# The output projection of a hybrid decoder layer in 512-column products by channel group, with the second half's residual rows placed behind the first half's norm

## The chip, the cores and the metric

The kernel runs on one core of a Trainium2 chip. The metric is the device time of one execution in microseconds (us). The core has a matrix engine (PE, whose weight loads are listed as PEld), a vector engine (DVE), an activation engine (ACT), a general engine (POOL) and a queue engine that issues DMAs (SP). Each engine works through its own list of instructions in order; an instruction waits there until the ones it depends on, on other engines, are done.

## The reference

One layer of a decoder with 1024 tokens and 1024 channels, all in float32. Cut to what matters here:

```python
proj = x @ w_in + b_in
q, k, v, a, gate = split(proj)                       # 512, 128, 128, 512, 512 columns
y_attn = sliding_window_gqa(q, k, v, sinks, table)   # 8 heads of 64, window 128, (1024, 512)
y_conv = conformer_conv_group(a, gate, ...)          # GLU, causal conv of 31, LayerNorm, silu, (1024, 512)
y   = concat([rms_norm(y_attn, attn_out_gain), rms_norm(y_conv, conv_out_gain)])
mix = y @ w_out + b_out                              # (1024, 1024) @ (1024, 1024)
x1  = layer_norm(alpha * x + mix, ln1_g, ln1_b)      # alpha = 2 ** 0.25
h   = causal_depthwise_conv(x1 @ w_up, ...)          # 5632 columns, conv of 3
g, u = split(h)
x   = layer_norm(alpha * x1 + (silu(g) * u) @ w_down, ln2_g, ln2_b)
```

The RMS norm of each group is one factor per token and one gain per channel. The gains are multiplied into the operands, and the factor per token can be applied after the product, separately for the 512 attention channels and the 512 conv channels.

## The kernel before

The 1024 tokens are worked on in two halves (H = 0 and 1) of 512 tokens, each in four blocks of 128 (t = 0 to 3). Every float32 matrix is split into a high and a low part of a shorter type: for weights, ACT casts the high part (line 236) and POOL subtracts it from the original (line 238). A product is then three matmuls: high by high, high by low, low by high.

A half goes through the input projection, the conv group (`conv`, `conv_norm`), the attention (`attn`), the output projection (`out_proj`), the first norm (`ln1`) and the feed-forward part. The conv group's end, `conv_norm`, subtracts the mean over channels (POOL's sums, line 466), multiplies by the deviation's inverse (DVE, line 489), applies silu (ACT, line 490, which needs its function table loaded), and makes the high part (ACT, line 491), the low part (DVE, line 492) and squares (ACT, line 495) for the RMS factor. The attention's units reduce the scores on DVE (line 533), take exponentials on ACT (line 540, another function table, with line 544 for the sinks), split the probabilities (ACT line 562, DVE line 563) and scale and split the result (ACT line 588, DVE line 590).

`out_proj(H)` first loads `b_out` to all partitions and the four rows blocks of x; DVE makes alpha * x + b_out of each (line 646, 128 x 1024), and this is the row block `acc` to which the products are added. Then it goes over four blocks of 256 output columns. For each it loads and splits the attention rows of `w_out` (`wa`, eight DMAs of 64 x 256, because the heads are paired) and the conv rows (`wc`, one DMA). For each t twelve matmuls of 256 columns (lines 661 to 663) make the attention group's product in one half of a PSUM bank, and twelve more (lines 665 to 667) the conv group's in the other half; DVE adds each to `acc` with its factor per token (`sA`, line 671; `sC`, line 673). The banks come from a pair with the tag A. In the first half, `chain` keeps the long products in the order in which they are written.

`ln1(0)` normalises a row block (`layer_norm_rows`: lines 321 and 323 statistics, 315 and 316 inverse root, 334 to 336 the row itself) and `transpose_split` turns it: PE transposes four 128 x 128 pieces into a bank (line 283), ACT casts them to the high part (line 286), DVE subtracts for the low part (line 287). This is done twice for each row block. The up products of the feed-forward part (lines 270, 271 and 273, in `mm3`; convolution and silu in lines 706 to 722) need all four row blocks. `ln1(1)` does the same for the second half in another form (transposes in line 297).

What sets the order: the parts are generators that yield after each piece of work, and a string names which one goes on next:

```python
SCRIPT = ('0hx00j0hxixxiiiggacaaaaaaaaaaaaannnCCaaagagCkCqqaaaqqoAAAoA'
          'AAAAoAAoNAlAlNAlAlNAAAAfAfAAOOOfsOsssffLLLLffff')
```

o is the first half's `out_proj`, l its `ln1`, A and N the second half's attention and conv norm, O and L its `out_proj` and `ln1`, f feed-forward work of the first half, s sums for the later joint stage. From about 498.5 us on both halves go through the feed-forward part together. A scheduler takes the instructions in this order as priorities, works out a schedule with its own cost model, and from it the list of each engine; a dependence added by hand (`add_manual_dep` with the class NoSync) binds only the order.

Of the kernel before, what the change touches and what calls it, by code (L numbers as in the profile page):

```python
# [15 lines left out]
P = 128  # L16
# [53 lines left out]
def hybrid_layer_kernel(  # L70
# [52 lines left out]
    last_tap = [None]  # L123

# [151 lines left out]
    def transpose_split(src, xh, xl, t, key):  # L276
        banks = []
        for q in range(2):
            b = psk(key)
            banks.append(b)  # L280
            for k in range(4):
                kt = q * 4 + k
                nc.tensor.transpose(out=b[:, k * P:(k + 1) * P], in_=src[:, kt * P:(kt + 1) * P], identity=ident)
            bv_ = b.rearrange("p (k t) -> p k t", t=P)
            hd = xh[q][:, :, t * P:(t + 1) * P]
            nc.scalar.copy(out=hd, in_=bv_)
            nc.vector.tensor_tensor(out=xl[q][:, :, t * P:(t + 1) * P], in0=bv_, in1=f(hd), op=ALU.subtract)  # L287
        return banks
# [328 lines left out]
    def wout_rows(c0, q0):  # L617
        def g(raw):
            r = []
            for j in range(4):  # L620
                c = c0 + j
                if c < 4:
                    for k in range(2):
                        rows = slice(k * 256 + c * HD, k * 256 + (c + 1) * HD)
                        r.append((raw[k * HD:(k + 1) * HD, j, :], w_out[rows, q0:q0 + 256]))
            if c0 >= 4:
                r = [(raw, w_out[c0 * P:(c0 + 4) * P, q0:q0 + 256].rearrange("(c p) n -> p c n", p=P))]
            return r
        return g

    def split_wout(c0, q0):
        return split_weights(wout_rows(c0, q0), (P, 4, 256), ("oh", "ol", "or"))
# [4 lines left out]
    def out_proj(H):  # L637
        ych, ycl = yC[H]
        bo = bcast_row(b_out, "bo")
        for t in range(TB):  # L640
# [4 lines left out]
            if XM[H]:  # L645
                nc.vector.scalar_tensor_tensor(out=a, in0=a, scalar=ALPHA, in1=bo, op0=ALU.mult, op1=ALU.add)
# [3 lines left out]
        for q in range(4):  # L650
            wa = split_wout(0, q * 256)
            wc = split_wout(4, q * 256)
            for t in range(TB):
                b = H * TB + t
                cs = slice(q * 256, (q + 1) * 256)
                yah, yal = yA[b]
                ts_ = slice(t * P, (t + 1) * P)
                pa = psk("out%d" % H, (P, 2, 256))
                m = []
                for c in range(4):  # L660
                    m.append(nc.tensor.matmul(out=pa[:, 0, :], lhsT=yah[:, c, :], rhs=wa[0][c], start=c == 0, stop=False))  # L661
                    m.append(nc.tensor.matmul(out=pa[:, 0, :], lhsT=yah[:, c, :], rhs=wa[1][c], start=False, stop=False))
                    m.append(nc.tensor.matmul(out=pa[:, 0, :], lhsT=yal[:, c, :], rhs=wa[0][c], start=False, stop=c == 3))
                for c in range(4):
                    m.append(nc.tensor.matmul(out=pa[:, 1, :], lhsT=ych[c][:, ts_], rhs=wc[0][c], start=c == 0, stop=False))
                    m.append(nc.tensor.matmul(out=pa[:, 1, :], lhsT=ych[c][:, ts_], rhs=wc[1][c], start=False, stop=False))
                    m.append(nc.tensor.matmul(out=pa[:, 1, :], lhsT=ycl[c][:, ts_], rhs=wc[0][c], start=False, stop=c == 3))
                if H == 0:
                    chain(m[0], m[-1])
                a = acc[b][:, cs]  # L670
                nc.vector.scalar_tensor_tensor(out=a, in0=pa[:, 0, :], scalar=sA[H][:, t:t + 1], in1=a,
                                               op0=ALU.mult, op1=ALU.add)
                nc.vector.scalar_tensor_tensor(out=a, in0=pa[:, 1, :], scalar=sC[H][:, t:t + 1], in1=a,
                                               op0=ALU.mult, op1=ALU.add)
            yield

    def ln1(H, g, b):
# [3 lines left out]
        for t in range(TB):  # L681
            a = acc[H * TB + t]
            if H == 0:
                layer_norm_rows(a, g, b, H)
                transpose_split(a, xh, xl, t, "ln0")
# [423 lines left out]
```

## Time and profile before

| | us |
|---|---|
| three runs | 1107.92, 1106.47, 1104.14 |
| median | 1106.47 |
| the profiled execution, its own time | 1105.66 |
| its span | 1103.9 |

Busy time in the span: PE 1047.1 us (95%), DVE 780.9, POOL 660.6, ACT 496.3. A share of 95% is a mean over stages: in some PE is full, in others DVE or a chain through several engines sets the pace. The views used below are the chain of waits (which work was last to end, followed backward), windows (busy time of each engine in a stretch), and timelines (single instructions with start, duration, and in brackets the idle time before them and what ended it). Where the profile groups neighbours, a row has a count (x4) and their busy time together. The second half's held rows of the change are the four of line 646 at 295.66 to 304.87 us.

### The profile page before, as it was taken

To read this page: it belongs to the slowest core of one execution; us is meant where nothing else is said; L and a number is where in the kernel's file an instruction comes from. 1 tells how busy PE (TensorE), PEld (TensorE's weight loads), DVE (VectorE), ACT (ScalarE), POOL (GpSimd) and SP (SyncE) were. 2 spreads that over 40 slices of the span, in tenths; PEclk is the share of its full clock that TensorE was granted. 3 is DMA by queue.
4 is the path that set the end of the run, shared out by engine and by line. 5 is a ranking of instruction groups with operands and counts; after the bars stand their busy time and mean duration, and the time that the engine had idled before them with its cause. 6 is when DMAs were issued, how large, how long until landed. Compare 5 with 4: busy or idle time off the path is not lost.

```text
span 1103.9 us, 14411 instructions
## 1 busy us (share of the span) xinstructions
PE 1047.1 (95%) x5113; PEld 872.3 (79%) x5113; DVE 780.9 (71%) x1426; ACT 496.3 (45%) x949; POOL 660.6 (60%) x564
## 2 busy tenths in 40 slices
PE   7999999988968999989999999999999999999996
PEld 5887778778957999767788787878787887888875
DVE  2999789999997447984747566565747466569666
ACT  4545677653458325662525242423425152442530
POOL 4759687874686555776646363737456463637551
PEclk9999999999968999999999999999999999999999
DMA  6535221423500242231212020211212110233321
GB/s 185 173 79 132 83 57 33 143 69 102 165 20 1 72 139 72 58 101 39 77 39 76 21 77 20 77 38 47 68 39 77 39 58 20 77 115 121 109 96 76
DMA packets 115673, 85.20 MB, mean 77 GB/s; under 512 B 20370, under 2 KB 108049, under 8 KB 115601
## 3 DMA queue, kind: packets, MB, share of 16 engines
q1 hardware_dynamic: 112368, 78.92, 24.2%
q10 hardware_dynamic: 3233, 5.36, 1.4%
q8 instruction: 40, 0.66, 0.3%
q14 instruction: 32, 0.26, 0.1%
HBM read 80.06 MB, written 4.21 MB: 76 GB/s over the span
## 4 chain that ended last, share of the span: by engine, by line
PE 77%; DVE 11%; POOL 4%; DMA 3%; ACT 3%; issue 1%; SPq 0%; POOLq 0%; ACTq 0%; DVEq 0%
PE psA L270 6%; PE psA L271 6%; PE psA L273 6%; PE psS L746 2%; PE psS L748 2%; PE psS L747 2%; PE psS L829 2%; PE psA L829 2%; PE psA L827 2%; PE psS L827 2%; PE psA L826 2%; PE psS L826 2%; PE psS L528 2%; DVE psC L444 1%; PE psA L661 1%
## 5 line engine op out<-in xcount | busy, mean ns | idle before, releaser
L238 POOL TENSOR_TENSOR wl<-raw,wh 128x512 fp32r<-128x512 f32 x196 | 260.1, 1339 | 139.0 <-ACT wh L236 67.4
L236 ACT CAST wh<-raw 128x512 fp32r<-128x512 f32 x196 | 119.2, 619 | 168.3 <-PE psA L271 19.9
L238 POOL TENSOR_TENSOR wl<-ts,wh 128x512 fp32r<-128x512 f32 x64 | 82.5, 1296 | 155.1 <-ACT wh L236 135.3
L444 DVE SCALAR_TENSOR_TENSOR psC<-hconv,const,psC 128x512 f32<-128x512 f32 x196 | 147.3, 752 | 3.5
L270 PE MATMUL psA<-x,wh 128*128 128x512 f32 x336 | 132.7, 395 | 4.4 <-ACT wh L236 3.5
L271 PE MATMUL psA<-x,wh 128*128 128x512 f32 x336 | 132.0, 393 | 1.4 <-DVE x L287 1.4
L236 ACT CAST wh<-ts 128x512 fp32r<-128x512 f32 x64 | 39.4, 622 | 177.4 <-PE psS L748 39.2
L273 PE MATMUL psA<-x,wl 128*128 128x512 f32 x336 | 87.2, 395 | 0.8 <-POOL wl L238 0.8
L270 PEld LDWEIGHTS psA<-x,wh 128*128 128x128 f32 x336 | 63.1, 188 | 19.1 <-ACT wh L236 4.1
L271 PEld LDWEIGHTS psA<-x,wh 128*128 128x128 f32 x336 | 63.1, 188 | 14.6 <-DVE x L287 1.7
L273 PEld LDWEIGHTS psA<-x,wl 128*128 128x128 f32 x336 | 62.4, 188 | 15.3 <-POOL wl L238 1.2
L316 POOL TENSOR_TENSOR tiny<-tiny,const 128x1 f32<-128x1 f32 (+1 forms) x28 | 26.0, 933 | 58.9 <-DVE tiny L315 55.9
L753 DVE TENSOR_TENSOR acc<-psS,acc 128x512 f32<-128x512 f32 x52 | 35.7, 688 | 31.6 <-PE psS L748 31.6
L238 POOL TENSOR_TENSOR ol<-or,oh 128x512 fp32r<-128x512 f32 x32 | 40.7, 1292 | 17.3 <-ACT oh L236 17.3
L826 PE MATMUL psA<-x,wh 128*128 128x512 f32 x112 | 43.6, 389 | 0.0
L827 PE MATMUL psA<-x,wh 128*128 128x512 f32 x112 | 43.6, 389 | 0.0
L826 PE MATMUL psS<-x,wh 128*128 128x512 f32 x112 | 43.6, 389 | 0.0
L827 PE MATMUL psS<-x,wh 128*128 128x512 f32 x112 | 43.6, 389 | 0.0
L865 POOL TENSOR_TENSOR ts<-raw,ts 128x512 f32<-128x512 f32 x32 | 41.9, 1310 | 1.3
L436 POOL TENSOR_TENSOR cp<-cp,cp 128x512 f32<-128x512 f32 x28 | 36.2, 1292 | 8.3 <-ACT cp L432 8.3
L746 PE MATMUL psS<-wh,gh 128*128 128x512 f32 x88 | 34.9, 397 | 6.3 <-ACT gh L726 3.9
L661 PE MATMUL psA<-oh,x 128*128 128x256 f32 x128 | 38.1, 297 | 1.8 <-ACT z L422 1.5
(394 smaller groups left out, 3081.1 us busy)
## 6 DMA issues: line engine op xcount, KB each, us to landing
raw<-in_w_up SPq DMA_DIRECT2D x56, 512.0 KB
raw<-in_w_down SPq DMA_DIRECT2D x28, 512.0 KB
raw<-in_w_in SPq DMA_DIRECT2D x20, 512.0 KB
raw<-in_x SPq DMA_DIRECT2D x8, 512.0 KB
raw<-in_w_in SPq DMA_DIRECT2D x16, 256.0 KB
acc<-in_x SPq DMA_DIRECT2D x8, 512.0 KB
or<-in_w_out SPq DMA_DIRECT2D x64, 64.0 KB
or<-in_w_out SPq DMA_DIRECT2D x8, 512.0 KB
```

What stands on the lines that cost most here:

```text
L236: nc.scalar.copy(out=h, in_=part)
L238: nc.gpsimd.tensor_tensor(out=l, in0=part, in1=f(h), op=ALU.subtract)
L270: m.append(nc.tensor.matmul(out=o, lhsT=wh[kt], rhs=xh[kt], start=kt == 0, stop=False))
L271: m.append(nc.tensor.matmul(out=o, lhsT=wh[kt], rhs=xl[kt], start=False, stop=False))
L273: m.append(nc.tensor.matmul(out=o, lhsT=wl[kt], rhs=xh[kt], start=False, stop=kt == KT - 1))
L444: tap(nc.vector.scalar_tensor_tensor(out=dst if k == KO else total, in0=src, scalar=cdw(k, c), in1=total, op0=ALU.mult, op1=ALU.add))
L661: m.append(nc.tensor.matmul(out=pa[:, 0, :], lhsT=yah[:, c, :], rhs=wa[0][c], start=c == 0, stop=False))
L746: m.append(nc.tensor.matmul(out=o, lhsT=gh[:, tsl], rhs=wh, start=j == 0, stop=False))
L826: m.append(nc.tensor.matmul(out=o, lhsT=wh[k], rhs=xh[k], start=k == 0, stop=False))
L827: m.append(nc.tensor.matmul(out=o, lhsT=wh[k], rhs=xl[k], start=False, stop=False))
L829: m.append(nc.tensor.matmul(out=o, lhsT=wl[k], rhs=xh[k], start=False, stop=k == 3))
L865: nc.gpsimd.tensor_tensor(out=t, in0=x0, in1=x1, op=ALU.subtract)
```

## The change

In `out_proj` the loop over four blocks of 256 columns becomes a loop over the channel group and two blocks of 512 columns: first the conv group's two blocks, then the attention group's two. Each t then has twelve matmuls of 512 columns into one full bank and one DVE eviction of 128 x 512 with that group's factor. The weights come in tiles of 128 x 2 x 512: one DMA for a conv tile, four of 64 x 512 for an attention tile. Per half that makes 192 matmuls instead of 384, 16 evictions instead of 32, and 20 DMAs of `w_out` instead of 36. `transpose_split` also returns its last subtract, and in `out_proj(1)` the four instructions that make alpha * x + b_out must stand behind the last such subtract of `ln1(0)` in DVE's list.

```diff
             bv_ = b.rearrange("p (k t) -> p k t", t=P)
             hd = xh[q][:, :, t * P:(t + 1) * P]
             nc.scalar.copy(out=hd, in_=bv_)
-            nc.vector.tensor_tensor(out=xl[q][:, :, t * P:(t + 1) * P], in0=bv_, in1=f(hd), op=ALU.subtract)
-        return banks
+            i = nc.vector.tensor_tensor(out=xl[q][:, :, t * P:(t + 1) * P], in0=bv_, in1=f(hd), op=ALU.subtract)
+        return banks + [i]
...
     def wout_rows(c0, q0):
         def g(raw):
+            if c0 >= 4:
+                return [(raw, w_out[c0 * P:(c0 + 2) * P, q0:q0 + 512].rearrange("(c p) n -> p c n", p=P))]
             r = []
-            for j in range(4):
-                c = c0 + j
-                if c < 4:
-                    for k in range(2):
-                        rows = slice(k * 256 + c * HD, k * 256 + (c + 1) * HD)
-                        r.append((raw[k * HD:(k + 1) * HD, j, :], w_out[rows, q0:q0 + 256]))
-            if c0 >= 4:
-                r = [(raw, w_out[c0 * P:(c0 + 4) * P, q0:q0 + 256].rearrange("(c p) n -> p c n", p=P))]
+            for j in range(2):
+                for k in range(2):
+                    r0 = k * 256 + (c0 + j) * HD
+                    r.append((raw[k * HD:(k + 1) * HD, j, :], w_out[r0:r0 + HD, q0:q0 + 512]))
             return r
         return g
 
     def split_wout(c0, q0):
-        return split_weights(wout_rows(c0, q0), (P, 4, 256), ("oh", "ol", "or"))
+        hs, ls = [], []
+        for c in (c0, c0 + 2):
+            h, l = split_weights(wout_rows(c, q0), (P, 2, 512), ("oh", "ol", "or"))
+            hs += h
+            ls += l
+        return hs, ls
...
             if XM[H]:
-                nc.vector.scalar_tensor_tensor(out=a, in0=a, scalar=ALPHA, in1=bo, op0=ALU.mult, op1=ALU.add)
+                i = nc.vector.scalar_tensor_tensor(out=a, in0=a, scalar=ALPHA, in1=bo, op0=ALU.mult, op1=ALU.add)
+                if H == 1:
+                    tc.add_manual_dep(i.ins, last_row[0].ins.name, order, reason="rows of one half at a time")
...
-        for q in range(4):
-            wa = split_wout(0, q * 256)
-            wc = split_wout(4, q * 256)
+        for part_, q in ((1, 0), (1, 1), (0, 0), (0, 1)):
+            wh, wl = split_wout(4 * part_, q * 512)
             for t in range(TB):
...
-                pa = psk("out%d" % H, (P, 2, 256))
+                if part_:
+                    yh, yl = [[y[c][:, ts_] for c in range(4)] for y in (ych, ycl)]
+                else:
+                    yh, yl = [[y[:, c, :] for c in range(4)] for y in yA[b]]
+                pa = psk("out%d" % H)
                 m = []
                 for c in range(4):
...
+                    m.append(nc.tensor.matmul(out=pa, lhsT=yh[c], rhs=wh[c], start=c == 0, stop=False))
+                    m.append(nc.tensor.matmul(out=pa, lhsT=yh[c], rhs=wl[c], start=False, stop=False))
+                    m.append(nc.tensor.matmul(out=pa, lhsT=yl[c], rhs=wh[c], start=False, stop=c == 3))
                 if H == 0:
                     chain(m[0], m[-1])
...
-                nc.vector.scalar_tensor_tensor(out=a, in0=pa[:, 1, :], scalar=sC[H][:, t:t + 1], in1=a,
-                                               op0=ALU.mult, op1=ALU.add)
+                a = acc[b][:, q * 512:(q + 1) * 512]
+                s = (sC if part_ else sA)[H]
+                nc.vector.scalar_tensor_tensor(out=a, in0=pa, scalar=s[:, t:t + 1], in1=a, op0=ALU.mult, op1=ALU.add)
             yield
...
-                transpose_split(a, xh, xl, t, "ln0")
+                last_row[0] = transpose_split(a, xh, xl, t, "ln0")[2]
```

In the changed kernel most lines have a number higher by one (287 is 288, 490 is 491, 540 is 541, 722 is 723); the residual rows are line 650 instead of 646, and the evictions line 675 instead of 671 and 673.

The first place where the order of instructions moves is DVE at the end of the first half's output projection, where its evictions (lines 671 and 673) and the first norm's statistics (lines 315, 321, 323) meet. Before (`acc_2114` and the next three are the first half's row blocks, `acc_3463` and the next the second half's):

```order
L671 SCALAR_TENSOR_TENSOR acc_2117<-psA,tiny_60,acc_2117 128x256
L323 BN_AGGR tiny_60<-tiny_60 128x2
L646 SCALAR_TENSOR_TENSOR acc_3463<-acc_3463,bo_3461 128x1024
L673 SCALAR_TENSOR_TENSOR acc_2117<-psA,tiny_60,acc_2117 128x256
L315 TENSOR_SCALAR tiny_60<-tiny_60 128x1
L321 BN_STATS tiny_60<-acc_2120 128x6
L646 SCALAR_TENSOR_TENSOR acc_3466<-acc_3466,bo_3461 128x1024
L671 SCALAR_TENSOR_TENSOR acc_2120<-psA,tiny_60,acc_2120 128x256
L321 BN_STATS tiny_60<-acc_2117 128x6
```

In the changed kernel these four rows stand on DVE at the end of the first norm, behind its last two subtracts (line 288; lines 493 are the conv norm's low parts, 538 and 546 attention):

```order
L288 TENSOR_TENSOR x_97<-psA,x_96 128x4x128
L538 TENSOR_TENSOR tiny_60<-const_61,tiny_60 128x4
L493 SCALAR_TENSOR_TENSOR x_95<-cy_1510,const_61,x_94 128x512
L316 TENSOR_SCALAR tiny_60<-psT 128x1
L493 SCALAR_TENSOR_TENSOR x_95<-cy_1511,const_61,x_94 128x512
L493 SCALAR_TENSOR_TENSOR x_95<-cy_1512,const_61,x_94 128x512
L288 TENSOR_TENSOR x_265<-psA,x_264 128x4x128
L650 SCALAR_TENSOR_TENSOR acc_3239<-acc_3239,bo_3237 128x1024
L650 SCALAR_TENSOR_TENSOR acc_3242<-acc_3242,bo_3237 128x1024
L650 SCALAR_TENSOR_TENSOR acc_3245<-acc_3245,bo_3237 128x1024
L650 SCALAR_TENSOR_TENSOR acc_3248<-acc_3248,bo_3237 128x1024
L546 TENSOR_TENSOR tiny_60<-tiny_60 128x4
```

The four rows moved as one group from among the evictions to behind the last subtract, and three of the conv norm's subtractions now stand ahead of that subtract.

The second place is ACT at the fourth row block's two casts (line 286, now 287, to `x_96` and `x_264`), where the conv norm's silus of the second half begin. Before:

```order
L286 CAST x_96<-psA 128x4x128
L490 ACT_TABLE_LOAD
L490 ACTIVATE cy_1510<-cy_1510,const_61 128x512
L286 CAST x_264<-psA 128x4x128
L686 ACTIVATE acc_2123<-acc_2123 128x1024
L490 ACTIVATE cy_1511<-cy_1511,const_61 128x512
L491 ACTIVATE x_94<-cy_1510,const_61 128x512
L495 ACTIVATE nsq_2938<-cy_1510 128x512
```

In the changed kernel, where the table for silu and two of the silus stand ahead of the first of these casts:

```order
L287 CAST x_96<-psA 128x4x128
L491 ACTIVATE cy_1512<-cy_1512,const_61 128x512
L492 ACTIVATE x_94<-cy_1510,const_61 128x512
L496 ACTIVATE nsq_2714<-cy_1510 128x512
L491 ACTIVATE cy_1513<-cy_1513,const_61 128x512
L492 ACTIVATE x_94<-cy_1511,const_61 128x512
L496 ACTIVATE nsq_2717<-cy_1511 128x512
L541 ACT_TABLE_LOAD
L541 ACTIVATE hank_262,tiny_60<-hank_262,tiny_60 128x256 x2
L492 ACTIVATE x_94<-cy_1512,const_61 128x512
L496 ACTIVATE nsq_2720<-cy_1512 128x512
L287 CAST x_264<-psA 128x4x128
```

Between the two casts one silu with its table load has become two silus, three pairs of lines 492 and 496, and a table load with two exponentials.

More of the change, by code (lines that the diff above doesn't have):

```diff
@@ L123, in hybrid_layer_kernel @@
     last_tap = [None]
+    last_row = [None]
     def tap(i):
@@ L649, in out_proj @@
                 nc.gpsimd.tensor_tensor(out=a, in0=a, in1=bo, op=ALU.add)
-        for q in range(4):
-            wa = split_wout(0, q * 256)
-            wc = split_wout(4, q * 256)
+        for part_, q in ((1, 0), (1, 1), (0, 0), (0, 1)):
+            wh, wl = split_wout(4 * part_, q * 512)
             for t in range(TB):
                 b = H * TB + t
-                cs = slice(q * 256, (q + 1) * 256)
-                yah, yal = yA[b]
                 ts_ = slice(t * P, (t + 1) * P)
-                pa = psk("out%d" % H, (P, 2, 256))
+                if part_:
[3 more added lines that the diff above has]
+                pa = psk("out%d" % H)
@@ L659, in out_proj @@
                 m = []
                 for c in range(4):
[L661 to L667, printed above, removed]
+                    m.append(nc.tensor.matmul(out=pa, lhsT=yh[c], rhs=wh[c], start=c == 0, stop=False))
@@ L668, in out_proj @@
+                    m.append(nc.tensor.matmul(out=pa, lhsT=yh[c], rhs=wl[c], start=False, stop=False))
+                    m.append(nc.tensor.matmul(out=pa, lhsT=yl[c], rhs=wh[c], start=False, stop=c == 3))
                 if H == 0:
                     chain(m[0], m[-1])
-                a = acc[b][:, cs]
-                nc.vector.scalar_tensor_tensor(out=a, in0=pa[:, 0, :], scalar=sA[H][:, t:t + 1], in1=a,
-                                               op0=ALU.mult, op1=ALU.add)
-                nc.vector.scalar_tensor_tensor(out=a, in0=pa[:, 1, :], scalar=sC[H][:, t:t + 1], in1=a,
-                                               op0=ALU.mult, op1=ALU.add)
+                a = acc[b][:, q * 512:(q + 1) * 512]
```

## The prediction

> **What bounds the kernel now.** I read the chain of waits first, then busy time by stage, then the order on single engines where a stage is not filled by one of them. The page's head, the rows of PE and its clock in forty slices, and the chain by engine:
>
> ```profile
> span 1103.9 us, 14411 instructions
> PE   7999999988968999989999999999999999999996
> PEclk9999999999968999999999999999999999999999
> PE 77%; DVE 11%; POOL 4%; DMA 3%; ACT 3%; issue 1%; SPq 0%; POOLq 0%; ACTq 0%; DVEq 0%
> ```
>
> PE carries 77% of the chain and DVE 11%. The slices in which PE drops to 8 and 6 and its clock to 6 and 8 lie at about 225 to 345 us, the end of the first half's output projection and the first norm. The same stretches by stage (columns: us, then busy time and count of PE, its weight loads, DVE, ACT, POOL; granted clock; DMA share; GB/s):
>
> ```profile
> core 0: us, PE busy (x) PEld busy (x) DVE busy (x) ACT busy (x) POOL busy (x), PEclk, DMA share, GB/s
> 208.13:225.92 17.79, 13.88 (x84) 12.16 (x83) 17.57 (x46) 13.37 (x37) 14.07 (x18) 0.89 0.40 119
> 225.92:311.08 85.16, 75.89 (x564) 69.94 (x564) 80.14 (x187) 37.26 (x105) 52.67 (x58) 0.96 0.32 100
> 311.08:344.93 33.85, 24.64 (x114) 20.14 (x113) 31.16 (x70) 23.16 (x49) 24.80 (x28) 0.70 0.05 16
> 345.00:372.50 27.50, 27.50 (x152) 23.79 (x151) 14.92 (x29) 17.27 (x32) 18.23 (x16) 1.00 0.17 49
> 372.50:427.00 54.50, 54.50 (x412) 52.48 (x411) 29.18 (x61) 15.18 (x25) 27.03 (x23) 1.00 0.34 103
> 427.00:498.50 71.50, 65.04 (x297) 52.63 (x296) 61.97 (x102) 49.72 (x95) 52.37 (x35) 1.00 0.25 74
> ```
>
> From 208.13 to 344.93 us (136.8 us) DVE is busy 17.57 + 80.14 + 31.16 = 128.9 us: here DVE sets the time, while PE has 22.4 us free. From 345 to 427 PE is busy in every microsecond. From 427 to 498.5, the second norm among the first products of the feed-forward part, neither is full: PE 65.04 and DVE 61.97 of 71.5. After that the change leaves the order of DVE's rows as it was, and PE's, ACT's and POOL's nearly; before 208 us too. So three stages need a price.
>
> **Evictions, first half.** DVE's two forms, by the distance of starts, since neighbours overlap by some 0.08 us:
>
> ```profile
> 225.92 0.47 DVE L671 SCALAR_TENSOR_TENSOR acc<-psA,tiny,acc 128x256 f32<-128x256 f32 x1
> 226.31 0.74 DVE L444 SCALAR_TENSOR_TENSOR psC<-hconv,const,psC 128x512 f32<-128x512 f32 x1
> 226.97 0.47 DVE L673 SCALAR_TENSOR_TENSOR acc<-psA,tiny,acc 128x256 f32<-128x256 f32 x1
> ```
>
> A 256-column eviction takes 226.31 − 225.92 = 0.39 us. A 512-column one is not in the trace; the nearest row, the same operation from and to a bank at 512 columns, takes 226.97 − 226.31 = 0.66. 32 × 0.39 − 16 × 0.66 = 1.9 us less DVE work in each half (two-sided bound: none, if it took 0.78, to 5.9 if 0.41).
>
> **The held rows.** The second half's four residual rows now stand among the first norm's work:
>
> ```profile
> 295.66 1.23 DVE L646 SCALAR_TENSOR_TENSOR acc<-acc,bo 128x1024 f32<-128x1024 f32 x1 [0.38 <-DMA acc<-in_x]
> 296.80 0.48 DVE L673 SCALAR_TENSOR_TENSOR acc<-psA,tiny,acc 128x256 f32<-128x256 f32 x1
> 297.86 1.21 DVE L646 SCALAR_TENSOR_TENSOR acc<-acc,bo 128x1024 f32<-128x1024 f32 x1
> 301.50 1.22 DVE L646 SCALAR_TENSOR_TENSOR acc<-acc,bo 128x1024 f32<-128x1024 f32 x1
> 303.63 1.32 DVE L646 SCALAR_TENSOR_TENSOR acc<-acc,bo 128x1024 f32<-128x1024 f32 x1
> ```
>
> 296.80 − 295.66 = 1.14; four are 4.6 us, and DVE stood 0.38 us for the first one's data. Both go to behind the last split of the first norm. Together with the evictions 1.9 + 4.6 + 0.4 = 6.9 us leave DVE's queue before that split. The new order also carries three of the conv norm's subtractions (line 492, 0.69 each by the 512-column subtract below) ahead of it, +2.1, and four attention products (line 590) and one subtract (line 563) behind it, −1.7. **DVE's path: −6.5 us.**
>
> But the last split needs a cast on ACT, and there the order changes too. ACT and DVE at that place now:
>
> ```profile
> 330.70 0.51 ACT L540 ACTIVATE hank<-hank,tiny 128x256 f32<-128x256 f32 x1
> 331.72 0.21 ACT L544 ACTIVATE tiny<-tiny 128x4 f32<-128x4 f32 x1
> 341.01 0.60 ACT L286 CAST x<-psA 128x512 fp32r<-128x512 f32 x1
> 341.63 1.28 ACT L490 ACT_TABLE_LOAD   x1
> 342.92 0.82 ACT L490 ACTIVATE cy<-cy,const 128x512 f32<-128x512 f32 x1
> 343.64 0.57 ACT L286 CAST x<-psA 128x512 fp32r<-128x512 f32 x1
> 345.07 0.81 ACT L490 ACTIVATE cy<-cy,const 128x512 f32<-128x512 f32 x1
> 345.78 0.71 ACT L491 ACTIVATE x<-cy,const 128x512 fp32r<-128x512 f32 x1
> 346.39 0.62 ACT L495 ACTIVATE nsq<-cy 128x512 f32<-128x512 f32 x1
> 336.34 1.12 DVE L590 SCALAR_TENSOR_TENSOR x<-psY,const,x 128x128 fp32r<-128x128 f32 x4
> 337.38 0.68 DVE L287 TENSOR_TENSOR x<-psA,x 128x512 fp32r<-128x512 f32 x1
> 339.72 0.69 DVE L563 TENSOR_TENSOR ph<-psT,ph 128x512 fp32r<-128x512 f32 x1
> 340.41 2.48 DVE L489 TENSOR_TENSOR cy<-cy,psN 128x512 f32<-128x512 f32 x4
> 344.24 0.69 DVE L287 TENSOR_TENSOR x<-psA,x 128x512 fp32r<-128x512 f32 x1 [0.76 <-ACT x L286]
> ```
>
> Now the fourth row's two casts stand 343.64 − 341.01 = 2.63 us apart, with one table load and one silu between. From the first multiply of line 489 to the end of the last split are 344.93 − 340.41 = 4.5 us. After the change ACT runs from the table load (1.28) through four silus (0.72 each, 342.92 to 343.64), three pairs of lines 491 and 495 (0.61 + 0.62, some 1.13 overlapped), a second load (1.28) for two exponentials (1.02, 330.70 to 331.72), the two casts (0.62 each) and the subtract (0.69): 1.28 + 2.9 + 3.4 + 1.28 + 1.0 + 1.2 + 0.7 = 11.8 us. That chain starts earlier, because less DVE work stands ahead of line 489: four held rows 4.6, evictions 1.9, four of line 590 1.0, two of line 563 1.2, two of line 287 1.2, two score reductions of line 533 some 0.9 (0.47 each): 10.8 us. **ACT's path: −10.8 + 11.8 − 4.5 = −3.5 us.** The later path decides: I take **−3.5**. Bounds: −6.5 if ACT is done in time; above, the last cast comes 2 × 0.72 + 3 × 1.13 + 1.28 + 1.02 + 0.62 = 7.7 behind the one before it instead of 2.63, **+5.1**, if the chain of line 489 starts no earlier.
>
> The load's row is 1.28 us and stands 0.02 us behind the cast's end (341.61); the silu follows 0.01 behind it. So I charge 1.28 for each. The Trainium skill's page "ScalarE: Activation LUTs", section "What ACT_TABLE_LOAD costs", states about 1283 ns for the load and about 1380 ns for a drain with every switch. No drain shows in the rows quoted, so the trace agrees with the load alone; by the page the two loads would cost an estimated 2.8 us more, and the total would be 1103.5.
>
> **345 to 372.5.** The held rows land here: 14.92 + 4.6 = 19.5 of DVE's 27.5 us, under a PE with 27.50 of 27.50. Behind them in DVE's queue wait the last attention unit's reciprocal and the up products' convolution rows. Price 0; without PE's cover 4.6. The second new table load stands here ahead of a feed-forward silu (line 722, now 723) on ACT, busy 17.27 of 27.5 us: 0, or 1.28 if that silu were waited for.
>
> **Products, second half (372.5 to 427).** PE is full, so the gap between matmuls counts:
>
> ```profile
> 423.89 0.28 PE L661 MATMUL psA<-oh,x 128*128 128x256 f32 x1
> 426.77 0.40 PE L270 MATMUL psA<-x,wh 128*128 128x512 f32 x1
> 432.24 0.60 PE L297 MATMUL psC<-const,acc 128*128 128x128 f32 x4
> 497.52 0.50 PE L746 MATMUL psS<-wh,gh 128*128 128x512 f32 x1 [3.27 <-ACT gh L726]
> ```
>
> The 24 matmuls of 256 columns from 423.89 take 2.88 us, 120 ns each; the 24 of 512 from 426.77 take 5.47, 228 ns each. One for two saves 12 ns; 192 times: **−2.3 us** (bounds 0, if weight loads set the pace, and −2.3). The first half's products save as much, but under DVE, with PE's 22.4 free us: 0. There the conv group now comes first and three attention score sets (six matmuls each) fall behind the projection into the norm's stretch, where PE is busy 24.64 of 33.85 us: 0 too. The evictions and the 16 DMA issues fewer in this half run beside a full PE: 0.
>
> **427 to 498.5.** Price 0, but the order around the second norm moves. Before, its last transposes (line 297) are followed by 64 up and 9 down matmuls; now by 27 up, 9 down, 12 and 27 more: 37 matmuls × 0.228 = 8.4 us more lie ahead of them. What waits on them comes 8.4 us later; they fill the 3.27 us in which PE waits at 497.52. Bounds: +5.1 (8.4 − 3.27) and −6.5 (71.5 − 65.04, all idle closed).
>
> **Sum:** −3.5 − 2.3 = −5.8 us. Against the profiled execution (1105.66, of which 1103.9 is the span) that is 1099.9; the median 1106.47 lies 0.8 above it, so **1100.7**.
>
> **Rivals.**
> - *All of it arrives.* ACT is done in time (−6.5), the products count (−2.3) and the wait at 497.52 closes (−3.3): −12.1, median 1094.4. For it: DVE's 128.9 of 136.8. Against: ACT's longer list.
> - *The second norm gives it back.* −3.5 − 2.3 + 5.1 = −0.7: 1105.8. For it: the 8.4 us; against: 64 up products were there as cover and 27 remain.
> - *Slower: the last cast is caught behind the conv norm's silus.* It decides if the first silu comes later than 344.93 − 11.8 = 333.1 us on the old scale. The conv norm's sums give a reason: POOL's two adds at 301.53 come after 3.56 us idle and so may not be DVE's to hurry:
>
> ```profile
> 301.53 4.54 POOL L466 TENSOR_TENSOR nsum<-cy,cy 128x512 f32<-128x512 f32 x2 [3.56 <-PE psA L663]
> 215.30:218.70 3.40, 3.40 (x17) 3.40 (x17) 3.18 (x9) 2.03 (x8) 3.40 (x4) 0.50 0.38 124
> ```
>
>  Then +5.1, during which PE idles ahead of the up products that need the fourth row, and a window like 215.3 to 218.7, 3.40 us at clock 0.50, costs 1.7 of PE. +5.1 + 1.7 − 2.3 = +4.5: 1111.0. Against: line 466 ran beside two held rows, which have left.
> - *A table load costs twice its row* where it stands between other functions: 2 × 1.28 more, 1103.3. By the quoted rows nothing of the kind shows. The Trainium skill's page "ScalarE: Activation LUTs", section "What ACT_TABLE_LOAD costs", names such a cost as a drain.
> - That the hold does nothing can be excluded: the order shows all four rows behind the last split.
>
> **How the numbers follow.** Forecast 0.42, all arrives 0.18, given back 0.18, slower 0.18, dear loads 0.04. The forecast's own range is 1097.5 (−6.5 − 2.3) to 1104. The 8-in-10 range reaches from 1093 (just under the first rival) to 1110.5, which leaves out most of the slower case's upper half. A measurement tells 0.3%, 3.3 us, from no change: faster is below 1103.2, slower above 1109.8. Forecast: 0.38 faster, 0.04 same; all arrives: 0.18 faster; given back: 0.03, 0.13, 0.02; slower case: 0.04 same, 0.14 slower; dear loads: 0.02 and 0.02. Faster 0.61, same 0.23, slower 0.16.
>
> **What would show it.** The last split of the first norm should end about 3.5 us earlier, near 341.4, with the cast (now line 287) as its releaser, and the first silu near 330. Then the first-half evictions at 0.66 us, the held rows at 342 to 348 without a wait of PE behind them, 24 matmuls in 5.47 us in the second half's projection, and the joint stage's start 5 to 6 us earlier than 498.5. I am wrong if ACT's list ends later than before, if PE has a wait where the fourth row's products begin, or if PE's idle between 421 and 493 grows beyond 6.5 us.

## The result and the profile after

The changed kernel takes 1098.74 us (median of 4 runs, 1097.0 to 1099.42) against 1107.2 for the kernel before (median of 4, with one run more than above): ratio 0.9917, 95% interval 0.9896 to 0.9937. Run again later, beside the last kernels below, it took 1100.43 us, ratio 0.9943 (0.9922 to 0.9964). The forecast was 1100.7, faster. Single executions lie 2 to 4 us around these medians, and the two intervals overlap.

The head of the page of the changed kernel, with its rows of PE and PE's clock, and its chain:

```profile
span 1095.2 us, 13540 instructions
PE   7999999989888999989999999999999999999996
PEclk9999999999868999999999999999999999999998
PE 78%; DVE 13%; ACT 3%; DMA 3%; POOL 1%; issue 1%; SPq 0%; POOLq 0%; ACTq 0%; DVEq 0%
```

The weak slices are still there. To see where the gain is, both executions are cut at the same five events: the end of the first half's residual rows on DVE (208.20 us before, 207.89 after), the conv norm's first multiply (line 489, now 490), the end of the first norm's last split, the end of the second projection on PE, and the first product of the joint stage. Windows of the kernel before (columns as in the prediction):

```profile
208.20:340.41 132.21, 111.18 (x740) 99.54 (x739) 125.03 (x296) 69.31 (x184) 90.35 (x99) 0.88 0.27 84
340.41:344.93 4.52, 3.16 (x21) 2.63 (x20) 3.77 (x7) 4.49 (x7) 1.20 (x2) 1.00 0.00 0
344.93:426.93 82.00, 82.00 (x562) 76.30 (x561) 44.08 (x89) 32.51 (x57) 45.25 (x37) 1.00 0.28 84
426.93:491.37 64.44, 61.25 (x283) 49.77 (x281) 55.74 (x94) 46.33 (x90) 47.60 (x31) 1.00 0.25 75
```

and of the changed kernel:

```profile
207.89:325.46 117.57, 104.64 (x523) 84.23 (x522) 112.48 (x260) 65.35 (x172) 85.01 (x94) 0.88 0.30 95
325.46:338.25 12.79, 7.34 (x38) 5.82 (x36) 8.75 (x19) 12.73 (x21) 1.87 (x2) 0.87 0.00 1
338.25:421.51 83.26, 82.47 (x376) 68.29 (x377) 46.36 (x75) 29.26 (x55) 47.98 (x42) 0.98 0.27 83
421.51:483.46 61.95, 60.82 (x282) 49.53 (x281) 54.16 (x101) 46.84 (x90) 45.26 (x31) 1.00 0.26 77
```

In what follows A is the stretch to the last split (the first two rows together), B the one to the end of the second projection, C the one to the joint stage. A went from 136.7 to 130.4 (−6.4), B from 82.0 to 83.3 (+1.3), C from 64.4 to 61.9 (−2.5): −7.6 in all. Within A, the first multiply came 14.6 us earlier, and 8.3 of them were lost again behind it, where ACT is busy 12.73 of 12.79 us. Behind the joint's start the engines' lists are nearly as before; the rest of the span differs there by under 1 us here, and by up to some 5 between executions of the kernels below.

Single instructions of the changed kernel around the last split (ACT, DVE, PE and POOL; the bracket is the idle time before and its releaser):

```profile
326.55 1.28 ACT L491 ACT_TABLE_LOAD   x1
327.85 1.52 ACT L491 ACTIVATE cy<-cy,const 128x512 f32<-128x512 f32 x2
329.27 0.56 ACT L287 CAST x<-psA 128x512 fp32r<-128x512 f32 x1
333.54 1.28 ACT L541 ACT_TABLE_LOAD   x1
336.97 0.56 ACT L287 CAST x<-psA 128x512 fp32r<-128x512 f32 x1
336.57 0.75 DVE L493 SCALAR_TENSOR_TENSOR x<-cy,const,x 128x512 fp32r<-128x512 f32 x1 [2.79 <-ACT x L492]
337.56 0.69 DVE L288 TENSOR_TENSOR x<-psA,x 128x512 fp32r<-128x512 f32 x1 [0.23 <-ACT x L287]
338.17 6.80 DVE L650 SCALAR_TENSOR_TENSOR acc<-acc,bo 128x1024 f32<-128x1024 f32 x4
337.58 0.51 PE L271 MATMUL psA<-x,wh 128*128 128x512 f32 x1 [2.26 <-ACT x L287]
339.80 4.10 POOL L457 TENSOR_TENSOR nsq<-nsq,nsq 128x512 f32<-128x512 f32 x2 [4.87 <-ACT nsq L496]
```

The two casts of the fourth row stand 7.7 us apart, as the order said, and the last one releases both the split on DVE and, after 2.26 us of waiting, PE. DVE, too, had waited 2.79 us for ACT just before. From the table load to the end of the split are 338.25 − 326.55 = 11.7 us; the forecast had 11.8. The silus follow the table load within 0.02 us. The drain that the Trainium skill's page "ScalarE: Activation LUTs", section "What ACT_TABLE_LOAD costs", puts beside a load does not show here either, and the list's 11.7 us have no room for two of them. The four held rows take 6.80 us here: the first two 1.22 each, the last two, beside POOL's adds, 2.31 each.

### The profile page after: what moved, and what is told of

The parts are those of the page before. It is cut to its first block, busy times and chain, and to the rows that moved or that the text cites. A ratio compares the mean times of both kernels' runs of the same rounds, so it can differ in the third digit from the quotient of the medians.

```text
span 1095.2 us, 13540 instructions
## 1 busy us (share of the span) xinstructions
PE 1045.6 (95%) x4729; PEld 852.7 (78%) x4729; DVE 773.6 (71%) x1394; ACT 499.5 (46%) x951; POOL 659.8 (60%) x564
## 4 chain that ended last, share of the span: by engine, by line
PE 78%; DVE 13%; ACT 3%; DMA 3%; POOL 1%; issue 1%; SPq 0%; POOLq 0%; ACTq 0%; DVEq 0%
PE psA L271 6%; PE psA L272 6%; PE psA L274 6%; PE psS L747 3%; PE psS L748 3%; PE psS L749 3%; DVE psC L445 2%; PE psS L830 2%; PE psA L828 2%; PE psA L827 2%; PE psS L827 2%; PE psS L828 2%; PE psA L830 2%; PE psS L529 2%; PE psA L669 1%; PE psA L670 1%
## 5 line engine op out<-in xcount | busy, mean ns | idle before, releaser
L271 PE MATMUL psA<-x,wh 128*128 128x512 f32 x336 | 134.3, 400 | 5.1 <-ACT x L287 2.3
L669 PE MATMUL psA<-ol,x 128*128 128x512 f32 x128 | 51.2, 400 | 1.6 <-POOL ol L239 1.6
L668 PE MATMUL psA<-oh,x 128*128 128x512 f32 x128 | 50.6, 398 | 1.3 <-ACT oh L237 0.8
L670 PE MATMUL psA<-oh,x 128*128 128x512 f32 x128 | 50.3, 393 | 0.0
```

The source lines that it names most:

```text
L271: m.append(nc.tensor.matmul(out=o, lhsT=wh[kt], rhs=xh[kt], start=kt == 0, stop=False))
L668: m.append(nc.tensor.matmul(out=pa, lhsT=yh[c], rhs=wh[c], start=c == 0, stop=False))
L669: m.append(nc.tensor.matmul(out=pa, lhsT=yh[c], rhs=wl[c], start=False, stop=False))
L670: m.append(nc.tensor.matmul(out=pa, lhsT=yl[c], rhs=wh[c], start=False, stop=c == 3))
```

## The experiments

All ratios are to the kernel before, measured beside it, with 95% intervals. The stretches A, B and C are cut in each kernel's trace at the events above. A trace is one execution, which can lie up to some 3 us off its kernel's median, so the ratio and the sum of a row need not agree.

| kernel (name in the expectations) | ratio | A | B | C | sum |
|---|---|---|---|---|---|
| before | 1 | 136.7 | 82.0 | 64.4 | 283.2 |
| changed | 0.9917 (0.9896 to 0.9937) | 130.4 | 83.3 | 61.9 | 275.6 |
| changed, again (after_again) | 0.9943 (0.9922 to 0.9964) | 130.4 | 83.3 | 61.9 | 275.6 |
| hold alone (hold_only) | 0.9971 (0.9959 to 0.9984) | 129.9 | 86.7 | 64.4 | 281.0 |
| wide products alone (wide_only) | 1.0045 (1.0031 to 1.0058) | 140.6 | 84.4 | 61.9 | 286.9 |
| wide alone, silus behind the last cast (wide_cast_first) | 0.9967 (0.9953 to 0.9981) | 134.3 | 82.3 | 61.9 | 278.5 |
| attention group first (attn_first) | 0.9963 (0.9949 to 0.9977) | 136.7 | 84.2 | 61.9 | 282.8 |
| hold, wide in the first half only (wide_h0) | 0.9990 (0.9977 to 1.0004) | 130.3 | 86.1 | 65.5 | 281.9 |
| hold, wide in the second half only (wide_h1) | 0.9934 (0.9913 to 0.9955) | 130.0 | 83.9 | 61.9 | 275.8 |
| rows cut short (rows_short) | 0.9947 (0.9929 to 0.9965) | 131.1 | 83.2 | 62.5 | 276.8 |
| rows held until the up products (rows_up) | 0.9965 (0.9950 to 0.9981) | 130.5 | 83.3 | 61.9 | 275.7 |
| silus behind the last cast (cast_first) | 0.9940 (0.9922 to 0.9959) | 124.5 | 90.8 | 61.9 | 277.2 |
| both of the last two (cast_rows_up) | 0.9954 (0.9938 to 0.9971) | 124.7 | 89.3 | 61.9 | 275.9 |
| both, and the sums of squares later (sums_later) | 0.9908 (0.9891 to 0.9925) | 126.0 | 86.5 | 61.9 | 274.3 |

**The hold alone.** The kernel before with this:

```diff
+                if H == 1:
+                    tc.add_manual_dep(i.ins, last_row[0].ins.name, order, reason="rows of one half at a time")
```

> The kernel before with the hold alone: products stay 256 columns wide. Theory (DVE's queue to the last split of the first norm decides): the four held rows and their 0.4 us of waiting leave it, no silu is moved ahead of the fourth row's casts in ACT's order, so the last split ends 4 to 5 us earlier than 344.9 and the time falls by 3.5 to 5 us, ratio 0.9955 to 0.997. Rival (the hold is of no use, since the gain is that of the wider products): the last split stays where it is within 1 us and the ratio is 0.999 to 1.001. Second rival (the rows cost PE something at their new place): last split 5 us earlier, but PE's stretch from there to the end of the second projection grows by 3 us, ratio about 0.998.

Its first two stretches:

```profile
208.04:337.92 129.88, 111.56 (x751) 100.38 (x749) 123.38 (x292) 70.86 (x183) 87.05 (x95) 0.89 0.28 86
337.92:424.63 86.71, 84.11 (x568) 77.37 (x569) 52.10 (x99) 35.19 (x63) 50.17 (x44) 1.00 0.27 80
```

The last split is 6.9 us earlier, more than the 5 expected, and 4.7 of them are lost in B. There PE is idle 86.71 − 84.11 = 2.6 us where it was never idle before, and busy 2.1 us more. The ratio lies between those of the theory and the second rival; the course is the second rival's, though whether the rows are to blame is for the runs below.

**Wide products alone.** The changed kernel without the hold:

```diff
-                if H == 1:
-                    tc.add_manual_dep(i.ins, last_row[0].ins.name, order, reason="rows of one half at a time")
```

> The change without its hold: 512-column products by channel group, residual rows as before. Theory: DVE loses 1.9 us of evictions, PE 2.3 us in the second projection, and the idle of the second norm closes by 2.5 us as in the changed kernel: ratio 0.994 to 0.996, and with hold_only the two gains add up to about the whole (8 us). Rival (products alone make the gain): ratio 0.991 to 0.993. Rival (the caught cast eats it): last split no earlier than 344, ratio 0.998.

It is slower than before, which neither theory nor rivals reached (the caught cast came nearest). Its first stretch and four rows of ACT and PE:

```profile
208.27:348.85 140.58, 111.19 (x555) 88.83 (x554) 126.58 (x284) 80.44 (x198) 93.42 (x100) 0.86 0.26 79
338.07 1.28 ACT L541 ACT_TABLE_LOAD   x1
339.87 0.56 ACT L287 CAST x<-psA 128x512 fp32r<-128x512 f32 x1
340.84 0.57 ACT L287 CAST x<-psA 128x512 fp32r<-128x512 f32 x1
345.14 0.58 PE L582 MATMUL psY<-ph,vpad 128*128 128x256 f32 x1 [5.77 <-ACT ph L563]
```

Here another row block's two casts, still ahead of the last row's, come only at 339.87 and 340.84 us, behind the silus, a table load and an exponential; two more casts follow at 346. PE waits 5.77 us, in the end for a cast of the attention (line 563, at 344.52 us on ACT), which is caught in the same list. So the hold, alone worth 0.3%, and the products, alone worth −0.45%, together give 0.6 to 0.8%. They do not add up: with the wide products alone, ACT's list is another one than with both, as these rows show.

**Wide alone, with the silus behind the last cast.** The same, and

```diff
-            nc.scalar.copy(out=hd, in_=bv_)
+            last_cast[0] = nc.scalar.copy(out=hd, in_=bv_)
...
-            nc.scalar.activation(out=y[c], in_=y[c], func=AF.Silu, bias=clb[c], scale=clg[c])
+            i = nc.scalar.activation(out=y[c], in_=y[c], func=AF.Silu, bias=clb[c], scale=clg[c])
+            if H == 1:
+                tc.add_manual_dep(i.ins, last_cast[0].ins.name, order, reason="first norm's casts come first")
```

> wide_only (wide products, no hold), with the silus behind the fourth row's last cast. wide_only was 0.45% slower than before, with the third row's casts at 340 and 341 us and PE idle for 5.8 us at 339. Theory (wide products alone lose because the casts are caught behind the conv norm's silus, not by the products): the last split falls from 348.9 to 342 or less, and the ratio to before is 0.994 to 0.998. Rival (the order of the rows on DVE, with the held rows among them, is what is late): last split within 2 us of 348.9 and ratio over 1.002.

A falls by 6.3 us to 134.3 (the split ends at 342.27), and the ratio from 1.0045 to 0.9967. The edit moves the silus in ACT's list and leaves the products as they are, so it is shown that this list, with the casts caught behind the silus, made the wide products slow. Which of the caught casts counts most, the norm's or the attention's, is not separated.

**The attention group first.** The changed kernel with

```diff
-        for part_, q in ((1, 0), (1, 1), (0, 0), (0, 1)):
+        for part_, q in ((0, 0), (0, 1), (1, 0), (1, 1)):
```

> The changed kernel with the attention group's blocks first and the conv group's after them, in both halves. Theory (the count of evictions and products and the place of the rows decide, the order of the groups only shifts which attention units fall behind): within 2.5 us of the changed kernel, ratio to before 0.990 to 0.994. Rival (the conv group first is what lets the first projection end 13.7 us earlier, because the attention rows are not yet there when it starts): the projection ends near 300 us instead of 289.4 and the ratio is 0.996 or more. In ACT's order two fewer table loads stand near the fourth row's casts, which speaks for up to 2.6 us less.

```profile
208.02:344.74 136.72, 114.15 (x554) 92.14 (x553) 122.91 (x281) 75.14 (x193) 85.66 (x99) 0.84 0.27 81
```

The rival was right in kind, with a ratio of 0.9963: in this trace A is as long as before the change, though DVE has hardly more work in it than in the changed kernel (122.91 against 112.48 + 8.75 = 121.2 us), and the first projection's last product ends at 301.9 us instead of 289.4. So the order of the groups, which the expectation's theory had taken for neutral, is a working part of the change. How much it is worth is less sure: the trace is that of the slowest of six executions (1106.79 us, median 1103.55), and the interval lies clear of the changed kernel's first measurement but overlaps the second.

**One half at a time.** The hold, and the wide loop in one half with the narrow loop of before in the other:

```diff
+        if H == 0:        # in the other kernel: H == 1
+            for part_, q in ((1, 0), (1, 1), (0, 0), (0, 1)):
...
+        else:
+            for q in range(4):
```

> The hold, wide products in the first half alone and narrow ones in the second. Theory: up to the last split like the changed kernel (338), then a second projection 2.3 us longer and a second norm as before the change: 4 to 5 us over the changed kernel, ratio 0.9945 to 0.9970. Rival: 2.3 us over it, ratio 0.9935 to 0.9945.

> The hold, narrow products in the first half and wide ones in the second alone. Theory (192 matmuls fewer save 12 ns each in the full stretch, and the changed order at the second norm closes 2.5 us of PE's idle): up to the second projection like hold_only (last split near 338), the projection 2 to 3 us shorter, the stretch behind it 62 instead of 64.4 us; 4 to 5 us below hold_only, ratio 0.9925 to 0.9940. Rival (the second norm's gain comes from the first half's order and not from this half): only 2.3 us below hold_only, ratio 0.9945 to 0.9955.

Stretches of the kernel that is wide in the first half only, then of the one that is wide in the second half only:

```profile
209.48:339.75 130.27, 112.28 (x559) 90.04 (x557) 121.30 (x277) 78.10 (x192) 87.03 (x96) 0.88 0.28 85
339.75:425.85 86.10, 85.19 (x568) 78.41 (x569) 52.15 (x97) 31.09 (x57) 48.45 (x42) 0.98 0.27 80
425.85:491.36 65.51, 61.23 (x281) 49.75 (x281) 55.62 (x94) 46.11 (x90) 47.61 (x31) 1.00 0.24 74
```

```profile
209.65:339.63 129.98, 108.81 (x751) 98.23 (x749) 123.03 (x292) 71.08 (x184) 86.77 (x95) 0.92 0.28 86
339.63:423.55 83.92, 81.41 (x376) 67.22 (x377) 46.41 (x77) 33.03 (x61) 49.51 (x44) 1.00 0.27 82
423.55:485.44 61.89, 60.76 (x281) 49.53 (x281) 55.35 (x101) 47.16 (x90) 45.32 (x31) 1.00 0.26 77
```

The kernel that is wide in the second half only came out as its theory had it: ratio 0.9934, 4.2 us below the hold alone. The other was slower than both of its expectations: ratio 0.9990, where the highest had 0.9970.

The two pairs price the wide products. With the first half fixed, the second half's cost of narrow ones in B is 86.1 − 83.3 = 2.8 (first half wide) and 86.7 − 83.9 = 2.8 us (first half narrow), where the forecast had 2.3. C is 61.9 in every kernel whose second half is wide but one (62.5 with the rows cut short, below). Where the second half is narrow it is 64.4 with a narrow first half and 65.5 with a wide one: 2.5 and 3.6 us more. So the second half's wide products bring 5.2 us with a narrow first half and 6.3 with a wide one, and with the hold they are the whole gain: that kernel's sum is 275.8 against 275.6, its ratio 0.9934. In the first half the wide products with the conv group ahead bring nothing: A is 130.3 with them and 129.9 without.

**What the held rows cost where they are.** The changed kernel with the four rows 8 columns wide, and with the rows held further, behind the first up product's last subtract:

```diff
-                i = nc.vector.scalar_tensor_tensor(out=a, in0=a, scalar=ALPHA, in1=bo, op0=ALU.mult, op1=ALU.add)
+                w = 8 if H else D
+                i = nc.vector.scalar_tensor_tensor(out=a[:, :w], in0=a[:, :w], scalar=ALPHA, in1=bo[:, :w], op0=ALU.mult, op1=ALU.add)
```

```diff
-        nc.vector.tensor_tensor(out=gl, in0=zu, in1=f(gh), op=ALU.subtract)
+        i = nc.vector.tensor_tensor(out=gl, in0=zu, in1=f(gh), op=ALU.subtract)
+        if H == 0 and c == 0:
+            last_row[0] = i
```

> The changed kernel with the four held rows cut to 8 of their 1024 columns (it leaves out alpha * x + b_out for the other columns of the second half). Theory (at their new place the rows cost nothing, as predicted): the stretch from the last split of the first norm to the end of the second projection stays at 83.3 us within 0.7 and the ratio to before at 0.990 to 0.993. Rival (the four rows, 6.8 us there instead of 4.6, hold up the attention's reciprocal and compete with POOL's sums of squares, and PE pays): the stretch falls by 2 to 4 us, POOL's two sums by 1.4 us, ratio 0.987 to 0.990.

> The changed kernel with the hold at a later place: the four rows stand behind the first up product's last subtract (about 358 us) instead of the last split (338). If the rows cost PE something where they stand now, this gives the same gain as rows_short, 2 to 4 us less than the changed kernel; if they cost nothing, it is equal to it within 1 us; if the second projection's evictions, from 372 us on, then wait for them, it is slower by 1 to 3 us.

B is 83.2 with the rows cut to nearly nothing and 83.3 with the rows later, as in the changed kernel with 83.3. Though they take 6.80 us of DVE, they cost PE nothing. In one thing the rival was right: POOL's two adds of line 457, 4.10 us beside the rows, take 1.28 each without them; but PE gains nothing by it. Neither ratio is distinguishable from the changed kernel's second measurement (the later rows' 0.9965 lies above the first); the gain that the rival promised is not there. What lengthens B in the kernel with the hold alone is therefore not shown to be the rows, and stays open.

**The last cast.** The changed kernel with the silus behind the last cast (the edit shown above), then with the rows held further as well:

> The changed kernel with one more order dependence: the second half's four conv-norm silus stand behind the fourth row's last cast on ACT. Theory (the last split waits for that cast, which stands behind the silus, their pairs and a table load): the cast moves from 337 to about 331, PE's wait of 2.3 us before the first up product's second half goes, with half a window of half clock: 3 to 5 us faster than the changed kernel, ratio to before 0.987 to 0.989. Rival (the silus' later end then holds up the second projection, which needs their parts, or the conv norm's statistics, so nothing is gained): ratio 0.991 to 0.993, with a wait of PE between 350 and 372.

> cast_first (silus behind the fourth row's last cast) with the rows behind the first up product's subtract. In cast_first PE waits 1.6 us at 345 and 347 us for POOL's sums of squares, and then runs 6.8 us at half clock. Theory (POOL's sums are late because the low parts of the conv norm, the rows and POOL's adds are crowded into 332 to 348 us): without the rows there, the low parts and the sums come 3 to 5 us earlier, PE does not wait and the clock stays whole: 4 to 6 us below cast_first, ratio to before 0.987 to 0.990, under the changed kernel. Rival (ACT's list, whose silus and pairs now start only at 332, is what makes the sums late): the waits and the half clock stay, ratio 0.992 to 0.995 as in cast_first.

Of the first, two stretches, one window in B and the row of PE ahead of it:

```profile
207.79:332.26 124.47, 104.48 (x548) 84.05 (x547) 120.01 (x275) 69.60 (x181) 85.57 (x95) 0.93 0.28 89
332.26:423.07 90.81, 88.13 (x389) 72.24 (x388) 48.42 (x79) 37.89 (x66) 48.15 (x44) 0.95 0.26 76
348.38 1.73 PE L460 MATMUL psN<-const,nsq 128*128 128x1 f32 x8 [0.92 <-POOL nsq L458]
349.50:354.60 5.10, 5.10 (x14) 4.13 (x15) 2.29 (x4) 1.18 (x2) 2.58 (x3) 0.50 0.00 0
```

The last split comes 5.9 us earlier, and B is 7.5 us longer. PE waits for the conv norm's sums of squares, whose inputs now start later on ACT, and then works at half clock in a place where it was full. Taking the rows out of the way shortens B to 89.3 and leaves waits of 0.39, 0.53 and 0.91 us and a stretch of half clock. So both rivals (what ACT's list now makes later holds up the sums) were right in kind, and both theories wrong about the gain, though their ratios, 0.9940 and 0.9954, lie a little above the rivals' ranges. The cast that stood late was cheap, because what stood ahead of it is wanted soon after.

**The sums later.** The kernel with both (silus behind the last cast, rows held further), and

```diff
+        if H == 0 and c == 1:
+            for j in late_sums[-TB:]:
+                tc.add_manual_dep(j.ins, last_bulk[0].ins.name, order, reason="sums behind the first up products")
```

where `late_sums` are the four matmuls of the sums of squares.

> The changed kernel itself, beside the three others of this group, as their reference. All theories: ratio to before 0.990 to 0.994. A ratio over 0.995 would mean that the first measurement stood at the fast end of its spread and that the kernels with a later hold or an earlier cast are its equals.

> cast_rows_up with the four matmuls of the conv norm's sums of squares behind the third up product instead of the second. In cast_rows_up PE waits 0.9 us for them at 350 us and then runs at half clock from 351.5 to 355. Theory (this wait is what brings the half clock): both go, 2 to 3 us below cast_rows_up, ratio to before 0.991 to 0.993. Rival (the half clock comes by what PE did before, not by this wait): the wait goes, a window of half clock stays between 345 and 360, and the gain is under 1 us, ratio 0.994 to 0.996.

The place on PE without this edit (rows held further, silus behind the cast), then with it:

```profile
351.26 1.05 PE L460 MATMUL psN<-const,nsq 128*128 128x1 f32 x8 [0.91 <-POOL nsq L458]
351.50:354.90 3.40, 3.40 (x15) 2.82 (x15) 2.68 (x6) 2.06 (x3) 3.40 (x4) 0.61 0.00 0
```

```profile
355.29 0.95 PE L461 MATMUL psN<-const,nsq 128*128 128x1 f32 x8
349.50:356.90 7.40, 7.40 (x43) 6.43 (x43) 6.57 (x11) 3.86 (x6) 4.05 (x4) 1.00 0.00 0
334.64:421.09 86.45, 84.45 (x390) 69.62 (x390) 47.06 (x79) 37.67 (x66) 48.39 (x44) 0.99 0.27 80
```

The changed kernel's second measurement, 0.9943, came out just above the range expected of it, so the first stood toward the fast end of its spread.

With the sums later, the wait of 0.91 us and the half clock are both gone, and B is 2.9 us shorter; A is 1.3 us longer, so the sum falls by 1.6. This kernel takes 1097.24 us (1097.0 to 1097.62, 5 runs), ratio 0.9908, against 1100.43 and 0.9943 for the changed kernel run beside it. Its median is the lowest of all; but its interval just touches that of the changed kernel run beside it and overlaps most of that of the first measurement, and the trace accounts for 1.3 of the 3.2 us (274.3 against 275.6). The rest is not seen in these stretches, and is not claimed. The theory was right in kind; its ratio of 0.991 to 0.993 was narrowly missed.

## Why the prediction came out

The time was forecast within 2 us, but from a sum whose parts are off in both directions, so that the closeness is in part luck.

- *DVE sets the time of the stretch to the last split.* Half right. The stretch fell by 6.4 us, close to DVE's path as priced (−6.5), but it ends in ACT's list, for which DVE waited 2.79 us shortly before: the closeness is chance.
- *ACT's path, −3.5.* Right as the path that decides, mis-sized in two terms; it measured −6.4. The list took 11.7 us, as priced (11.8), and the last cast released the split. But the sum left out the 326.55 − 325.46 = 1.1 us from the first multiply to the table load, so 12.8 us stand against the 4.5 of before (+1.0). And the start, "10.8 us" for "less DVE work stands ahead of line 489", came 14.6 earlier (−3.8). DVE's busy time ahead of it fell by 12.5 and its idle time by 2.1. Groups of DVE ahead of the first multiply, of before and then of after:

```profile
L336 DVE TENSOR_TENSOR acc<-acc,bo 128x1024 f32<-128x1024 f32 x4 | 8.1, 2019 | 0.6 <-POOL acc L335 0.6
L671 DVE SCALAR_TENSOR_TENSOR acc<-psA,tiny,acc 128x256 f32<-128x256 f32 x16 | 7.6, 476 | 0.6 <-PE psA L667 0.6
```

```profile
L337 DVE TENSOR_TENSOR acc<-acc,bo 128x1024 f32<-128x1024 f32 x4 | 5.8, 1444 | 0.0
L675 DVE SCALAR_TENSOR_TENSOR acc<-psA,tiny,acc 128x512 f32<-128x512 f32 x16 | 11.9, 741 | 0.0
```

  The same four additions of the norm (line 336, now 337) became 2.3 us cheaper, a change of duration in instructions that nobody touched. The evictions' means, 476 and 741 ns, answer to the two rows on which they were priced.
- *Evictions of the first half, 1.9.* Right as a sum of work; but wide in the first half alone, with the hold, A is no shorter (130.3 against 129.9). There too PE waits 2.26 us for the fourth row's last cast, so the caught cast probably takes their place; that is argued, not shown.
- *The held rows cost nothing at their new place.* Right, although they take 6.8 us rather than 4.6: without them B is 83.2 instead of 83.3.
- *Products of the second half, −2.3.* Right in kind: the narrow products cost 2.8 us more of B in two pairs. But B as a whole grew by 1.3 instead of falling by 2.3. Of these 3.6 us, PE's idle time is 0.8 (83.26 − 82.47), and the clock, at half from 338.25 to 341.65 us where it had been whole, is a mean of 0.98 over 83 us, 1.7. The rest was not followed up.
- *The stretch of the second norm, 0 (bounds −6.5 and +5.1).* This term failed: −2.5 in the changed kernel. The last transposes did fall back, nearly as worked out:

```profile
472.68 0.60 PE L297 MATMUL psC<-const,acc 128*128 128x128 f32 x4
```

```profile
474.81 0.60 PE L298 MATMUL psC<-const,acc 128*128 128x128 f32 x4
```

  That is 45.8 us behind the second projection before and 53.3 after, 7.5 us (8.4 forecast). PE did not wait longer for it: its idle time in C fell from 3.2 to 1.1 us. The largest wait before, right behind these transposes and for a weight cast on ACT, is gone; why the new order brings that cast in time was not followed up. The wait that the prediction named, at 497.52 us, lies behind C and stayed, with 2.93 instead of 3.27 us. The largest wait in C before, then the named wait after:

```profile
474.69 0.50 PE L270 MATMUL psA<-x,wh 128*128 128x512 f32 x1 [1.41 <-ACT wh L236]
```

```profile
490.21 0.80 PE L747 MATMUL psS<-wh,gh 128*128 128x512 f32 x1 [2.93 <-ACT gh L727]
```

  The rival in which the gain is given back there had the move right and its sign wrong.
- *All of it arrives.* This rival's −6.5 and −3.3 are not far from what A and C did (−6.4 and −2.5), but not by its reasons: ACT was not done in time, and the wait at 497.52 did not close.
- *The slower rival, the last cast caught behind the silus.* The mechanism is real: it makes the wide products without the hold 0.45% slower. In the changed kernel it takes 8.3 of 14.6 us, but the first silu, at 327.85 us, came ahead of the 333.1 from which it would have decided. One sign of being wrong did appear, a wait of PE where the fourth row's products begin: 2.26 us at 337.58, where it had been 1.36 before. It lies in A, which ended earlier all the same.

Two failed terms, −2.9 (ACT's path) and −2.5 (second norm), and one loss of 3.6 in B in part cancel: −5.8 forecast to the joint stage, −7.6 measured.

## What to carry to other kernels

When a schedule is written by a scheduler, two edits that are each cheap on their own engine can meet in the list of a third: read the order of every engine on the chain's end, and price the in-order queue there, not the engine that is busiest. An instruction that stands late in a queue is worth moving only if what it passes is not wanted at the same time; here that took two more moves. Give an edit its price per half or per stage by making it in one stage alone: that showed that half of this change carried all of its products' gain.

## What had not been expected of the hardware

DVE and POOL slowed each other where both worked. One of the changed kernel's held rows with POOL idle, one beside POOL's adds of line 457, and all four in the kernel that holds them until the up products, where POOL is idle:

```profile
338.17 1.22 DVE L650 SCALAR_TENSOR_TENSOR acc<-acc,bo 128x1024 f32<-128x1024 f32 x1
340.43 2.31 DVE L650 SCALAR_TENSOR_TENSOR acc<-acc,bo 128x1024 f32<-128x1024 f32 x1
```

```profile
354.44 4.62 DVE L650 SCALAR_TENSOR_TENSOR acc<-acc,bo 128x1024 f32<-128x1024 f32 x4
```

POOL's two adds took 4.10 us beside the rows and 1.28 each without them. The norm's additions, 2.0 us on the mean before the change and 1.4 after it, fit this. It is not always DVE that pays: before the change the held rows at 301.50 and 303.63 us took 1.22 and 1.32 beside POOL's two adds of line 466, and there the adds were long, 4.54 us. That no other cause plays in is not shown.

PE's clock also fell to half after waits that were far shorter than the stretch of half clock: in the kernel with the silus behind the last cast and the rows held further, waits of 0.39, 0.53 and 0.91 us between 347 and 352 us were followed by some 3.4 us of it. With the sums later, waits of 0.24 and 1.03 us stand there, and the clock stayed whole. The length of the waits alone does not decide it. In the kernel with the hold alone PE was idle for 4.00 − 2.30 = 1.7 us in the first of these stretches, nearly as much as those 1.8 together, and the clock stayed whole in the second:

```profile
347.00:351.00 4.00, 2.30 (x15) 1.77 (x14) 3.89 (x8) 3.85 (x7) 4.00 (x5) 1.00 0.00 0
351.00:358.00 7.00, 7.00 (x41) 6.09 (x40) 4.38 (x8) 1.87 (x3) 4.53 (x5) 1.00 0.00 0
```

What else decides is not known from these runs. Between the two kernels with and without the half clock, B differs by 2.9 us.
